# Broadcasting the mLSTM decay rows on GpSimd, folding the sample normaliser into the state matmul, and keeping one output weight in SBUF

## The chip, the cores and the metric

The kernel runs on one core of a Trainium2 chip. The metric is the device time of one launch in microseconds (us). A profiled execution carries timestamps for every instruction on the five engines: TensorE (PE, and PEld for its weight loads), VectorE (DVE), ScalarE (ACT), GpSimd (POOL) and SyncE (SP, which issues all DMAs here).

## The reference, cut to what matters

One layer of a hybrid decoder: 2048 prompt tokens plus 16 meta tokens (one sequence), and 32 sample tokens (8 streams of 4) that start from a stored state. An mLSTM group (4 heads of 128) and a sliding-window attention group (8 heads of 64) share one input projection and one output projection. The mLSTM part, in chunks of 128 tokens:

```python
def mlstm_chunk(state, q, k, v, log_i, log_f):
    c, n, m = state
    b = jnp.cumsum(log_f, axis=1)
    dmat = b[:, :, None, :] - b[:, None, :, :] + log_i[:, None, :, :]
    dmat = jnp.where(causal, dmat, -jnp.inf)
    inter = b + m[:, None, :]
    m_t = jnp.maximum(inter, jnp.max(dmat, axis=2))
    w = jnp.exp(dmat - m_t[:, :, None, :])
    s_inter = jnp.exp(inter - m_t)
    qk = jnp.einsum('bthd,bshd->btsh', q, k) * w
    num = jnp.einsum('btsh,bshd->bthd', qk, v) + jnp.einsum('bthk,bhkv->bthv', q, c) * s_inter[..., None]
    den = jnp.sum(qk, axis=2) + jnp.einsum('bthk,bhk->bth', q, n) * s_inter
    h = num / jnp.maximum(jnp.abs(den), jnp.exp(-m_t))[..., None]
    ...
    c_new = decay[..., None, None] * c + jnp.einsum('bsh,bshk,bshv->bhkv', w_state, k, v)
    n_new = decay[..., None] * n + jnp.einsum('bsh,bshk->bhk', w_state, k)

# per layer
mq, mk, mv, mo, mz, mi, mf, aq, ak, av, az = split_proj(hp @ w_in[l] + b_in[l])
mix = concatenate([y_m, y_a]) @ w_o            # y_m, y_a: the two groups, gated
out = layer_norm(DN_ALPHA * x + mix, g, b)
```

The prompt runs through `mlstm_chunk` 16 times with the carried state; the sample streams run once, from `state_mlstm_c` and `state_mlstm_n`.

## The kernel before, in words

All large products run on TensorE as pairs of float16 pieces (high and low parts, three products each), with the weights split on the chip. The kernel has two phases over the 16 chunks of 128 prompt tokens.

**Phase A** (`a_steps`, up to about 553 us of the profile) does, for chunk n: the gates (`a_gate`), the projections q, k, v, o with weights `w_q`, `w_k`, `w_v`, `w_o` (`a_proj`, 24 matmuls each, lines 296 to 299), the mLSTM itself, and the layer norm of the input two chunks ahead (`load_x`, `norm_x`). Everything phase B needs goes to DRAM (`xT_d`, `h_d`, `hn_d`). Between the steps, a generator `jobs` is advanced by `pace(0.8)`: it handles the sample streams (`d_prepare`, `d_head`, then the attention of the sample tokens), and prepares the weights of phase B, which are written to DRAM (`spill`) and read back later (`reload`).

**Phase B** (from about 553 us) does, for block n: projections aq, kv, az, z with reloaded weights `wr_aq`, `wr_kv`, `wr_az`, `wr_z`; the scores (`s_unit`, line 1259), the transposes of the probabilities by DMA, the product with the values (`s_pv`, lines 1301 and 1312); the output projection of an earlier block (`b_out`, line 1339) and the final layer norm.

The weights lie in the pool `wp` of 5 buffers of 2 MB, tag "w". In phase A four of them hold `w_q`, `w_k`, `w_v`, `w_o`; the fifth passes from one job to the next. PSUM has 8 banks: `pj` 2 (projections), `pt` 3, `po` 2, `px` 1 (sample jobs).

**The decay rows.** In `m_rows` (line 753) VectorE makes a tile `M` (`rM`) whose rows 0, 32, 64 and 96 hold one head each, with the tokens along the free axis. `m_weights` needs each of these rows on all 128 partitions: `Mb`, 128 x 4 x 128. Before, TensorE does that with a constant `sel` (one row of ones per head), four float32 matmuls into a `pt` bank (line 762). Readers of `Mb` are `ws` (line 772), the weights `wt` (line 776) and `SI` (ACT, line 778); `SI` scales the queries `qs` on POOL (line 787), after POOL has added the two halves of `qT` (line 786). `d_prepare` does the same once for the sample tokens (line 656).

**The sample normaliser.** In `d_head` the state `C` (8 streams, 128 x 128) and the normaliser `E.nS` (a column per stream) are separate, so every stream takes a matmul of 128 columns (line 702) and one of a single column (line 703).

Who orders the work: the text above gives the program, but a list scheduler with a model of the engines then sets the order of the instructions on each engine, and tiles are placed in buffers in that order. DMAs all go through SP's queue, in order.

Of the kernel before, what the change touches and what calls it, by code (L numbers as in the profile page):

```python
# [16 lines left out]
P = 128  # L17
# [24 lines left out]
def tile_hymba_step(  # L42
# [109 lines left out]

    G.load_library(library_config.standard)
    ones = cst.tile([P, P], F32, name="ones")
# [52 lines left out]
    swamask = cs[:, C_SWA:C_SWA + 2 * NW].rearrange("p (i k) -> p i k", k=NW)  # L207
    sel = cst.tile([P, H, P], F32, name="sel")
    G.memset(sel, 0.0)
    for h in range(H):  # L210
        G.memset(sel[32 * h:32 * h + 1, h], 1.0)
    Gf = [cst.tile([P, P], F32, name=f"Gf{i}") for i in range(2)]
# [434 lines left out]
    def d_prepare():  # L647

        E.nS, E.nn = ea.take(NS), ea.take(NS)
        dma(E.nS, st_n)  # L650
        E.em = ea.take(4)[:NS]
        A.activation(E.em, tok[:NS, 1, :], AF.Exp, scale=-1.0)
        Mb5 = ea.take(160).rearrange("p (h b s) -> p h b s", h=H, s=5)
        ps = pt([P, H, 40])
        for h in range(H):
            T.matmul(ps[:, h], sel[:, h], M5, start=True, stop=True)
        A.activation(Mb5.rearrange("p h b s -> p (h b s)"), ps.rearrange("p h t -> p (h t)"), AF.Copy)
        E.SI = ea.take(128).rearrange("p (h b s) -> p h b s", h=H, s=4)
        for h in range(H):
            V.tensor_tensor(E.SI[:, h], Mb5[:, h, :, 0:1].to_broadcast([P, 8, 4]), Mb5[:, h, :, 1:5], op=ALU.subtract)  # L660
        A.activation(E.SI, E.SI, AF.Exp)
        yield
        E.We = ea.take(128)[:NS].rearrange("p (h t) -> p h t", h=H)
        for h in range(H):
            V.scalar_tensor_tensor(v4(E.We[:, h]), Mb5[:NS, h, :, 1:5], tok[:NS, 0, h:h + 1], v4(scaus[:NS]),
                                   op0=ALU.subtract, op1=ALU.max)
        A.activation(E.We, E.We, AF.Exp, scale=-1.0)
        wa = Arena(wp.tile([P, 4096], F32, tag="w", name="da"))
        E.C = [wa.take(1024) for _ in range(2)]
        E.kz = wa.take(1024)[:NS]  # L670
        E.eh = wa.take(4 * 129)[:NS].rearrange("p (c d) -> p c d", d=129)
        E.Zq = wa.take(288)
        G.memset(E.Zq, 0.0)
        G.memset(E.eh[:, 2, 128:129], 1.0)
        E.qkT = ea.take(64).rearrange("p (c t) -> p c t", t=NS)
        E.A = ea.take(32)[:NS]
        E.g = ea.take(128)[:NS]
        E.kw = ea.take(128)[:NS]
        E.den = ea.take(1)[:NS]

    def d_head(h):

        eh, C = E.eh, E.C[h % 2]
        dma(eh[:, :, 0:P], e_d[0:NS, :, h * P:(h + 1) * P])
        C3 = v3(C)
        dma(C3, st_c[:, h].rearrange("b k v -> k b v"))
        ps = px([P, 2, P])
# [12 lines left out]
        for b in range(8):  # L700
            z = E.Zq[:, b * NS:(b + 1) * NS]
            T.matmul(ps[:NS, :128], z, C3[:, b], start=False, stop=False, skip_group_check=True)
            T.matmul(ps[:NS, 128:129], z, E.nS[:, b * H + h:b * H + h + 1], start=False, stop=(b == 7),
                     skip_group_check=True)
        yield
# [13 lines left out]
        dec = E.SI[:, h, :, 3]  # L719
        G.tensor_tensor(C3, C3, dec.unsqueeze(2).to_broadcast([P, 8, P]), op=ALU.mult)  # L720
        nn = E.nn.rearrange("p (b h) -> p h b", h=H)[:, h]
        V.tensor_tensor(nn, E.nS.rearrange("p (b h) -> p h b", h=H)[:, h], dec, op=ALU.mult)
        for b0 in range(0, 8, 3):
# [3 lines left out]
            for i in range(nb):  # L727
                T.matmul(ps[:, i], kz[:, b0 + i], eh[:, 2], start=True, stop=True, skip_group_check=True)
            V.tensor_tensor(C3[:, b0:b0 + nb], C3[:, b0:b0 + nb], ps[:, :nb, 0:P], op=ALU.add)
            V.tensor_tensor(nn[:, b0:b0 + nb], nn[:, b0:b0 + nb], ps[:, :nb, 128], op=ALU.add)  # L730
        dma(sc[:, h].rearrange("b k v -> k b v"), C3)
        if h == H - 1:
# [5 lines left out]
    def m_rows(n):  # L738
# [14 lines left out]
        V.scalar_tensor_tensor(M, r2[:, 1], carry.m, b, op0=ALU.subtract, op1=ALU.subtract)  # L753
        c.r2, c.M = r2, M
        carry.m = r2[:, 1, P - 1:P]

    def m_weights(n):
        c = ca[n]
        r2 = c.r2
        Mb = pt([P, H, P])  # L760
        for h in range(H):
            T.matmul(Mb[:, h], sel[:, h], c.M, start=True, stop=True)
        ptr = pt([P, 2, P])
# [273 lines left out]
    def x_out(i):  # L1037
        wB[f"o{i}"] = w = W()
        yield from prep_steps(w, f"o{i}", ahead[f"o{i}"], 512, mg=mg, sums=range(4))
        if i == 0:  # L1040
            fetch("o1")
        spill(w, f"o{i}")
        yield
# [38 lines left out]
    def a_steps(n):  # L1082
# [285 lines left out]
    for n in range(NCH - 1):  # L1368
# [135 lines left out]
```

## Time and profile before

| | us |
|---|---|
| three timed runs | 1099.37, 1101.61, 1102.27 (median 1101.61) |
| the profiled execution: its time | 1096.6 |
| its span, first to last instruction | 1094.8 |
| PE busy in the span | 1039.4 (95%) |
| DVE / ACT / POOL busy | 735.2 / 443.3 / 262.9 |
| mean granted TensorE clock | 0.984 of full speed |

In the rows of the profile, a line such as "L762 PE MATMUL pt<-rM,sel" names the line of the kernel, the engine, the operation, the tile written and the tiles read; after it stand the shapes and the count. Matmuls overlap one another, so the duration of one (285 ns, say) is longer than its distance to the next; what a matmul costs is read from the distance between starts.

### The profile page before, as it was taken

Reading aid. Unit: us, or ns where it says so; the run is one execution under the profiler, and the core shown is the slowest. Engines: PE = TensorE matmul, PEld = TensorE weight load, DVE = VectorE, ACT = ScalarE, POOL = GpSimd, SP = SyncE. Lnnn points to the kernel's source line nnn. Section 1 sums busy time; section 2 is a strip of 40 time slices with the busy share of each in tenths; the row PEclk is TensorE's granted clock in tenths of the full one; section 3 lists DMA queues with packets and bytes.
Section 4 is the critical chain, followed back from the end, with each engine's and each line's share of the span. In section 5 each row is a group of like instructions: output and inputs, shape, how many; then the busy total and the mean of one; then the engine's idle time right before and its main releaser. Section 6 shows DMA issues by size and latency. Waiting matters only on the chain.

```text
span 1094.8 us, 17806 instructions
## 1 busy us (share of the span) xinstructions
PE 1039.4 (95%) x6455; PEld 577.1 (53%) x6455; DVE 735.2 (67%) x2069; ACT 443.3 (40%) x1108; POOL 262.9 (24%) x270
## 2 busy tenths in 40 slices
PE   7969999999989999889998999999999999999986
PEld 3425565565556555445564554555555555555543
DVE  6769676776766777866655676566666656667664
ACT  5646333235434344562225344343344333344430
POOL 2113232121111111101311332233332233332222
PEclk9989999999999999999999999999999999999998
DMA  9746545445974568478585555656555464544552
GB/s 321 197 129 174 148 129 119 109 119 135 292 171 124 127 218 240 131 224 288 206 280 101 117 115 131 127 119 120 127 94 134 123 139 115 123 105 108 109 106 76
DMA packets 246098, 166.04 MB, mean 152 GB/s; under 512 B 207977, under 2 KB 220985, under 8 KB 244441
## 3 DMA queue, kind: packets, MB, share of 16 engines
q1 hardware_dynamic: 246010, 164.90, 58.9%
q8 instruction: 51, 0.84, 0.3%
q14 instruction: 37, 0.30, 0.1%
HBM read 70.32 MB, written 45.68 MB: 106 GB/s over the span
## 4 chain that ended last, share of the span: by engine, by line
PE 59%; DMA 15%; DVE 13%; ACT 6%; issue 5%; POOL 2%; SPq 1%; DVEq 0%; ACTq 0%; POOLq 0%
PE pj L1339 14%; PE pj L297 11%; PE pj L296 11%; PE pj L299 11%; DMA xT<-hl 3%; PE pt L1259 2%; DMA EE<-stg 2%; PE po L1312 2%; DMA stg<-in_dram 2%; DVE xs L380 1%; DMA stg<-hl 1%; DMA wd_z<-w_z 1%; DMA wd_o<-w_o 1%; ACT hl L321 1%; PE po L826 1%
## 5 line engine op out<-in xcount | busy, mean ns | idle before, releaser
L1339 PE MATMUL pj<-wr_o,EE 128*128 128x512 f16 x720 | 166.9, 381 | 3.0 <-DMA EE<-stg 1.5
L296 PEld LDWEIGHTS <-xT 128*128 128x128 f16 x992 | 97.9, 99 | 103.1 <-issue 6.9
L297 PEld LDWEIGHTS <-xT 128*128 128x128 f16 x992 | 97.8, 99 | 97.3 <-issue 6.8
L299 PEld LDWEIGHTS <-xT 128*128 128x128 f16 x992 | 96.8, 98 | 97.8
L1339 PEld LDWEIGHTS <-EE 128*128 128x128 f16 x720 | 70.5, 98 | 81.1 <-DMA EE<-stg 3.4
L325 POOL TENSOR_TENSOR lns<-lns,mhalf 128x1 f32<-128x1 f32 (+1 forms) x16 | 21.3, 1332 | 175.5 <-ACT lns L324 158.7
L1268 DVE TENSOR_TENSOR hl<-g,hl 128x512 f16<-128x512 f32 (+1 forms) x32 | 23.2, 724 | 49.1 <-ACT hl L1267 49.1
L1272 POOL TENSOR_TENSOR mhl<-g,mhl 128x32 f16<-128x32 f32 x32 | 18.8, 587 | 145.1 <-ACT mhl L1271 145.1
L296 PE MATMUL pj<-w_q,xT 128*128 128x512 f16 x120 | 47.1, 392 | 6.0 <-DMA xT<-hl 6.0
L1272 POOL TENSOR_TENSOR mhl<-SI,mhl 128x32 f16<-128x32 f32 x32 | 18.5, 578 | 139.1 <-ACT mhl L1271 139.1
L1266 ACT ACTIVATE g<-g,nb 128x272 f32<-128x272 f32 (+1 forms) x64 | 32.4, 507 | 46.3 <-DVE nb L1263 46.3
L296 PE MATMUL pj<-wr_z,xT 128*128 128x512 f16 x128 | 48.8, 381 | 0.0
L297 PE MATMUL pj<-wr_z,xT 128*128 128x512 f16 x128 | 48.7, 380 | 0.0
L296 PE MATMUL pj<-w_v,xT 128*128 128x512 f16 x120 | 46.3, 386 | 2.4 <-DVE q L431 2.4
L296 PE MATMUL pj<-wr_az,xT 128*128 128x512 f16 x128 | 48.5, 379 | 0.0
L296 PE MATMUL pj<-wr_aq,xT 128*128 128x512 f16 x128 | 48.5, 379 | 0.0
L297 PE MATMUL pj<-wr_aq,xT 128*128 128x512 f16 x128 | 48.5, 379 | 0.0
L297 PE MATMUL pj<-wr_az,xT 128*128 128x512 f16 x128 | 48.5, 379 | 0.0
L787 POOL TENSOR_TENSOR qs<-qs,SI 128x512 f32<-128x512 f32 x16 | 23.8, 1486 | 98.2 <-ACT SI L778 98.1
L297 PE MATMUL pj<-w_q,xT 128*128 128x512 f16 x120 | 47.0, 392 | 0.0
L297 PE MATMUL pj<-w_v,xT 128*128 128x512 f16 x120 | 46.5, 388 | 0.0
L297 PE MATMUL pj<-w_o,xT 128*128 128x512 f16 x120 | 46.5, 388 | 0.0
(459 smaller groups left out, 2510.4 us busy)
## 6 DMA issues: line engine op xcount, KB each, us to landing
stg<-in_dram SPq DMA_DIRECT2D x28, 512.0 KB
xs<-in_dram SPq DMA_DIRECT2D x16, 512.0 KB
h_d<-xs SPq DMA_DIRECT2D x16, 512.0 KB
xT_d<-xT SPq DMA_DIRECT2D x16, 512.0 KB
xs<-h_d SPq DMA_DIRECT2D x16, 512.0 KB
xT<-xT_d SPq DMA_DIRECT2D x16, 512.0 KB
out_dram<-xs SPq DMA_DIRECT2D x15, 512.0 KB
hn_d<-g SPq DMA_DIRECT2D x16, 258.0 KB
```

What stands on the lines that cost most here:

```text
L296: T.matmul(ps, xT[:, k, :], w.t[:, k, 0, :n], start=(k == 0), stop=False)
L297: T.matmul(ps, xT[:, k, :], w.t[:, k, 1, :n], start=False, stop=False)
L299: T.matmul(ps, xT[:, KT + k, :], w.t[:, k, 0, :n], start=False, stop=(k == KT - 1))
L321: A.activation(junk[:, 0:D], x, AF.Copy, accum_out=sm)
L325: G.tensor_tensor(rs, ve, mhalf[:rows, 0:1], op=ALU.pow)
L787: G.tensor_tensor(c.qs, c.qs, c.SI, op=ALU.mult)
L1259: T.matmul(ps[:, lo:], c.qT[:, h], kTs[:, 2 * (h // 4) + x, lo:], start=(x == 0), stop=(x == 1))
L1266: A.activation(p[:, i, lo:], p[:, i, lo:], AF.Exp, bias=nb[:, h:h + 1], accum_out=sums[:, h:h + 1])
L1268: V.tensor_tensor(hl[:, 1, 2 * q:2 * q + 2, lo:], p[:, :, lo:2 * P], hl[:, 0, 2 * q:2 * q + 2, lo:], op=ALU.subtract)
L1272: G.tensor_tensor(m[:, 1], p[:, :, 2 * P:], m[:, 0], op=ALU.subtract)
L1312: T.matmul(pso[:, h], l, r, start=False, stop=(i == len(last) - 1), skip_group_check=True)
L1339: T.matmul(ps, c.yT[:, a, :], w[:, k, t, :], start=(first and j == 0), stop=(last and j == len(mm) - 1))
```

## The change

The change has these parts.

1. The four selector matmuls per chunk become four `G.partition_broadcast` instructions on GpSimd (from row 32h of `M` to all partitions of `Mb`), issued in `m_rows`; `Mb` now lies in SBUF. The same in `d_prepare`, where the copy out of PSUM goes too. The constant `sel` goes. GpSimd loads another library of its routines at the start.
2. In `d_head` the state tile gets a 129th column per stream, which holds the normaliser. The product with the queries, the decay and the update then cover it in the same instructions; the single-column matmuls go.
3. `x` of chunk n+3 is loaded in step n, before the norm of n+2. Step n has one `yield` less, and the job generator is advanced at 0.92 instead of 0.8 per yield.
4. The second half of the output weights, `w_o1`, is not written to DRAM and reloaded: it stays in its `wp` buffer. `wr_aq` therefore has to take another buffer.
5. `b_out(0)` moves from the end of block 1 into block 2, ahead of that block's scores.

```diff
-    G.load_library(library_config.standard)
+    G.load_library(library_config.all_libraries[10])
...
-        ps = pt([P, H, 40])
         for h in range(H):
-            T.matmul(ps[:, h], sel[:, h], M5, start=True, stop=True)
-        A.activation(Mb5.rearrange("p h b s -> p (h b s)"), ps.rearrange("p h t -> p (h t)"), AF.Copy)
+            G.partition_broadcast(Mb5[:, h].rearrange("p b s -> p (b s)"), M5[32 * h:32 * h + 1], channels=P)
...
-        C3 = v3(C)
-        dma(C3, st_c[:, h].rearrange("b k v -> k b v"))
+        C3 = C.rearrange("p (b d) -> p b d", d=129)
+        dma(C3[:, :, 0:P], st_c[:, h].rearrange("b k v -> k b v"))
+        V.tensor_copy(C3[:, :, P], E.nS.rearrange("p (b h) -> p h b", h=H)[:, h])
...
-            T.matmul(ps[:NS, :128], z, C3[:, b], start=False, stop=False, skip_group_check=True)
-            T.matmul(ps[:NS, 128:129], z, E.nS[:, b * H + h:b * H + h + 1], start=False, stop=(b == 7),
-                     skip_group_check=True)
+            T.matmul(ps[:NS, :129], z, C3[:, b], start=False, stop=(b == 7), skip_group_check=True)
...
-        c.r2, c.M = r2, M
+        Mb = work("Mb", [P, H, P])
+        for h in range(H):
+            G.partition_broadcast(Mb[:, h], M[32 * h:32 * h + 1], channels=P)
+        c.r2, c.Mb = r2, Mb
...
-        Mb = pt([P, H, P])
-        for h in range(H):
-            T.matmul(Mb[:, h], sel[:, h], c.M, start=True, stop=True)
+        Mb = c.Mb
...
-        spill(w, f"o{i}")
+        if i == 0:
+            spill(w, "o0")
...
-            xs, carry.mark = load_x(n + 2)
-            yield
+            if n == 0:
+                carry.xs, carry.mark = load_x(2)
+                yield
+            xs = carry.xs
+            if n + 3 < NCH:
+                carry.xs, carry.mark = load_x(n + 3)
             xTs[n + 2] = norm_x(n + 2, xs)
...
-            if pace(0.8):
+            if pace(.92):
...
-    for nm in ("az", "z", "o0", "o1"):
+    for nm in ("az", "z", "o0"):
         reload(wB[nm], nm)
...
+        if n == 2:
+            b_out(0)
         s_start(n)
...
-        elif n < NCH - 2:
+        elif 1 < n < NCH - 2:
             b_out(n - 1)
```

Four places show what the scheduler makes of it. The new kernel is a few lines shorter: its lines 748, 779, 780 and 758 are lines 753 and after, 786, 787 and 765 of the kernel before; a POOL row "ISA Mb<-rM" is a broadcast.

On PE, in chunk 0 behind the projection v, before (line 762 and 656: the selectors; 765: transposes of other rows):

```order
L762 MATMUL pt<-rM,sel 128x128 x4
L765 MATMUL pt<-cs,r_712 128x128 x2
L656 MATMUL pt<-ea,sel 128x40 x4
L299 LDWEIGHTS xT
L299 MATMUL pj<-w_v,xT 128x512
```

and now:

```order
L296 LDWEIGHTS xT
L296 MATMUL pj<-w_v,xT 128x512
L758 MATMUL pt<-cs,r_706 128x128 x2
L790 LDWEIGHTS kT
L790 MATMUL pt<-qT,kT 128x128
```

The eight selector matmuls are gone from PE's row of work, and nothing stands in their place.

On POOL, in chunk 1 (717 and 720 before, 711 and 714 now, belong to the sample head; 325 and 322 are the power of the layer norm of x), before:

```order
L786 TENSOR_TENSOR qs<-qT 128x512
L717 TENSOR_TENSOR da<-ea,cs 32x1024
L325 TENSOR_TENSOR lns<-lns,mhalf 128x1
L720 TENSOR_TENSOR da<-da,ea 128x1024
L497 TENSOR_TENSOR hn<-hn,mhalf 32x1
L787 TENSOR_TENSOR qs<-qs,SI 128x512
```

and now:

```order
L779 TENSOR_TENSOR qs<-qT 128x512
L711 TENSOR_TENSOR da<-ea,cs 32x1024
L748 ISA Mb<-rM 128x128 x4
L780 TENSOR_TENSOR qs<-qs,SI 128x512
L322 TENSOR_TENSOR lns<-lns,mhalf 128x1
L714 TENSOR_TENSOR da<-da,ea 128x1032
```

The broadcasts stand behind the addition of the two halves of `qT`, which waits for a DMA transpose and for the previous chunk's use of `qs`; the multiplication by `SI`, which needs them, follows.

On SP, at the end of phase A, before (the first `qT` and `kT` are chunk 14's):

```order
L103 DMA wr_aq<-wd_aq 128x8192
L103 DMA wr_kv<-wd_kv 128x4096
L103 DMA xs<-ze_d 32x1024
L103 DMA xs<-h_d_149 128x1024
L103 DMA_TRANSPOSE qT<-qh 128x8x128
L103 DMA_TRANSPOSE kT<-kh 128x8x128
L103 DMA hn_d_178<-g 128x516
L103 DMA xT<-xT_d_133 128x2048
L103 DMA out_dram<-xs 32x1024
L103 DMA xs<-h_d_150 128x1024
L103 DMA wr_az<-wd_az 128x8192
```

and now (the `qT` and `kT` in these rows are chunk 15's):

```order
L103 DMA wr_aq<-wd_aq 128x8192
L103 DMA bias<-in_dram 128x512
L103 DMA_TRANSPOSE qT<-qh 128x8x128
L103 DMA hn_d_173<-g 128x516
L103 DMA out_dram<-r_5370 1x1 x4
L103 DMA wr_az<-wd_az 128x8192
L103 DMA bias<-in_dram 128x256
L103 DMA_TRANSPOSE kT<-kh 128x8x128
L103 DMA wr_z<-wd_z 128x8192
```

The reload of `wr_aq` stands where that of `wr_az` stood, behind chunk 15's projection q, whose buffer it takes; before, it stood a chunk earlier.

On ACT, in phase B when the scores of block 1 are made (1314 before, 1312 now: the result of `s_pv(0)`; 988 and 981: gates; 1266 and 1264: the exponentials of the scores), before:

```order
L1232 ACTIVATE At<-At,hnb,hn 128x128 x4
L988 ACTIVATE kw<-kT 128x512
L1314 ACTIVATE stg<-qT 128x512
L1266 ACTIVATE g,sums<-g,nb 128x272 x2
L1267 ACTIVATE hl<-g 128x512
```

and now:

```order
L1230 ACTIVATE At<-At,hnb,hn 128x128 x4
L1264 ACTIVATE g,sums<-g,nb 128x272 x2
L981 ACTIVATE kw<-qs 128x512
L1265 ACTIVATE hl<-g 128x512
L1269 ACTIVATE mhl<-g 128x32
L1312 ACTIVATE stg<-qT 128x512
```

The result of `s_pv(0)` now comes behind the first scores of block 1, not ahead of them.

More of the change, by code (lines that the diff above doesn't have):

```diff
@@ L207, in tile_hymba_step @@
     swamask = cs[:, C_SWA:C_SWA + 2 * NW].rearrange("p (i k) -> p i k", k=NW)
-    sel = cst.tile([P, H, P], F32, name="sel")
-    G.memset(sel, 0.0)
-    for h in range(H):
-        G.memset(sel[32 * h:32 * h + 1, h], 1.0)
     Gf = [cst.tile([P, P], F32, name=f"Gf{i}") for i in range(2)]
@@ L668, in d_prepare @@
         wa = Arena(wp.tile([P, 4096], F32, tag="w", name="da"))
-        E.C = [wa.take(1024) for _ in range(2)]
+        E.C = [wa.take(8 * 129) for _ in range(2)]
         E.kz = wa.take(1024)[:NS]
@@ L719, in d_head @@
         dec = E.SI[:, h, :, 3]
-        G.tensor_tensor(C3, C3, dec.unsqueeze(2).to_broadcast([P, 8, P]), op=ALU.mult)
-        nn = E.nn.rearrange("p (b h) -> p h b", h=H)[:, h]
-        V.tensor_tensor(nn, E.nS.rearrange("p (b h) -> p h b", h=H)[:, h], dec, op=ALU.mult)
+        G.tensor_tensor(C3, C3, dec.unsqueeze(2).to_broadcast([P, 8, 129]), op=ALU.mult)
         for b0 in range(0, 8, 3):
@@ L728, in d_head @@
                 T.matmul(ps[:, i], kz[:, b0 + i], eh[:, 2], start=True, stop=True, skip_group_check=True)
-            V.tensor_tensor(C3[:, b0:b0 + nb], C3[:, b0:b0 + nb], ps[:, :nb, 0:P], op=ALU.add)
-            V.tensor_tensor(nn[:, b0:b0 + nb], nn[:, b0:b0 + nb], ps[:, :nb, 128], op=ALU.add)
-        dma(sc[:, h].rearrange("b k v -> k b v"), C3)
+            V.tensor_tensor(C3[:, b0:b0 + nb], C3[:, b0:b0 + nb], ps[:, :nb], op=ALU.add)
+        dma(sc[:, h].rearrange("b k v -> k b v"), C3[:, :, 0:P])
+        A.activation(E.nn.rearrange("p (b h) -> p h b", h=H)[:, h], C3[:, :, P], AF.Copy)
         if h == H - 1:
@@ L759, in m_weights @@
         r2 = c.r2
-        Mb = pt([P, H, P])
-        for h in range(H):
-            T.matmul(Mb[:, h], sel[:, h], c.M, start=True, stop=True)
+        Mb = c.Mb
         ptr = pt([P, 2, P])
```

## The prediction

> **What bounds the kernel now.** I read the busy shares first, then the stretches, then PE's waits, then single places in the timeline.
>
> ```profile
> PE 1039.4 (95%) x6455; PEld 577.1 (53%) x6455; DVE 735.2 (67%) x2069; ACT 443.3 (40%) x1108; POOL 262.9 (24%) x270
> 20.00:553.00 533.00, 502.60 (x3016) 286.40 (x3015) 383.22 (x1088) 228.05 (x486) 95.86 (x71) 0.98 0.63 177
> 553.00:618.00 65.00, 61.05 (x367) 34.44 (x365) 41.45 (x149) 28.11 (x89) 11.25 (x21) 0.97 0.64 163
> 618.00:1040.00 422.00, 420.51 (x2774) 228.22 (x2773) 270.29 (x745) 166.24 (x485) 136.56 (x146) 1.00 0.54 119
> PE pj L296 <- DMA xT<-hl: 6.0, 1, 6.0
> PE px L728 <- DVE ea L707: 3.3, 3, 1.6
> PE pt L135 <- ACT SI L778: 2.9, 1, 2.9
> PE po L1312 <- DMA stg<-hl: 3.0, 2, 2.4
> ```
>
> The first row gives TensorE 95% of the span. The three stretches (length, then PE, PEld, DVE, ACT, POOL busy, then the granted TensorE clock) are phase A, the start of phase B, and steady phase B. PE is idle 30.4 us in phase A (533.0 less 502.6), 4.0 us at the start of B, and 1.5 us in the 422 us after it. The waits of PE (total, times, longest) are short and have many causes. So the time is PE's work plus a few stalls: a microsecond of matmul taken out of phase A is worth close to 502.6/533.0 = 0.94 us, and a stall is worth its length plus what the clock loses behind it. DVE, at 383 of 533 us, is the next engine, with room.
>
> **The selectors (part 1).** Their price is the distance between starts, not the 285 ns of one:
>
> ```profile
> L762 PE MATMUL pt<-rM,sel 128*128 128x128 f32 x128 | 17.9, 285 | 0.0
> 233.56 1.16 PE L762 MATMUL pt<-rM,sel 128*128 128x128 f32 x8
> 234.55 0.38 PE L765 MATMUL pt<-cs,r 128*128 128x128 f32 x2
> 94.58 0.98 PE L656 MATMUL pt<-ea,sel 128*128 128x40 f32 x8
> 95.62 0.83 PE L797 MATMUL pt<-qT,kT 128*128 128x128 f16 x12
> ```
>
> A chunk's block of 8 records (4 matmuls) starts at 233.56 and the next work at 234.55: 0.99 us. 128 records are 16 such blocks: 15.8 us. The sample block goes from 94.58 to 95.62: 1.0 us. Both leave PE's path for good: nothing takes their place in PE's order.
>
> **Their new price on POOL.** The trace has no broadcast. The nearest rows of POOL:
>
> ```profile
> L218 POOL MEMSET Gf<- 128x128 f32 x2 | 0.4, 205 | 0.0
> L846 POOL TENSOR_TENSOR kd<-kvu,kd 128x128 f16<-128x128 f32 x32 | 15.4, 499 | 6.3 <-ACT kd L844 6.1 <-POOL hl L1274 0.2
> L325 POOL TENSOR_TENSOR lns<-lns,mhalf 128x1 f32<-128x1 f32 (+1 forms) x16 | 21.3, 1332 | 175.5 <-ACT lns L324 158.7 <-ACT am L767 16.9
> 16.81 0.60 POOL L325 TENSOR_TENSOR lns<-lns,mhalf 48x1 f32<-48x1 f32 x1 [9.56 <-ACT lns L324]
> ```
>
> A fill of 128x128 is 0.2 us, an operation with two inputs of that size 0.5 us, a software routine (a power of one element) up to 1.33 us. One broadcast is thus between 0.2 and 1.33 us; I take 0.5 us, the row with the same shape, so 2.0 us for four. What stands behind them is the reader:
>
> ```profile
> 531.21 0.34 DVE L753 SCALAR_TENSOR_TENSOR rM<-r,r,rb 128x128 f32<-128x128 f32 x1
> 535.97 0.16 DVE L772 TENSOR_TENSOR ws<-am,pt 128x4 f32<-128x4 f32 x1 [1.36 <-ACT am L767]
> 264.08 0.34 DVE L753 SCALAR_TENSOR_TENSOR rM<-r,r,rb 128x128 f32<-128x128 f32 x1
> 270.61 0.15 DVE L772 TENSOR_TENSOR ws<-am,pt 128x4 f32<-128x4 f32 x1
> 279.39 1.78 POOL L786 TENSOR_TENSOR qs<-qT 128x512 f32<-128x512 f16 x1 [13.37 <-DMA qT<-qh]
> ```
>
> `M` is ready at 531.55 and its first reader runs at 535.97: 4.4 us go to PE's turn and the evictions today. Four broadcasts of 0.5 us need 2.0, so they hide in it; at 1.33 us (5.3) VectorE would wait 0.9 us a chunk. If they hide, the cost is zero; that cover ends at 1.1 us each. The load of POOL's routine library, new too, comes once at the start, where POOL waited 9.56 us ahead of its first power (the row at 16.81); I count 0. DVE reads `Mb` from SBUF instead of PSUM; the 0.34 us of line 753, with its inputs in SBUF, is the size of that, off PE's path.
>
> The Trainium skill, page "GPSIMD Engine Reference", section "Specifications", says GpSimd shares its SBUF interfaces with VectorE and contends with vector instructions that use two ports or two SBUF inputs. The trace agrees as far as it goes: the same power took 0.60 us at 16.81 and 1.33 us on average. By that rule a broadcast would come to about 1.1 us (an estimate, 0.5 times 1.33/0.60), four to 4.4 us, just the cover, and the sum would stay but without margin.
>
> **PSUM (part 1).** `Mb` held one of three `pt` banks until `SI` was made. Once that stopped PE:
>
> ```profile
> 485.18 0.49 PE L135 MATMUL pt<-dg,ones 128*128 128x128 f32 x2 [2.90 <-ACT SI L778]
> 480.00:490.00 10.00, 6.80 (x39) 3.04 (x38) 8.35 (x22) 6.97 (x21) 2.60 (x2) 0.83 0.64 184
> PE pt L511 <- ACT SI L778: 0.4, 1, 0.4
> ```
>
> 2.9 and 0.4 us of waiting, and in that stretch the clock is 0.83 over 10 us, so 1.7 us lost: together 5.0 us. Between 0 (another bank or VectorE is late next, DVE being busy 8.35 of those 10 us) and 5.0, I take half, 2.5.
>
> **The normaliser (part 2).**
>
> ```profile
> L703 PE MATMUL px<-ea,da 128*32 128x1 f32 x64 | 6.3, 168 | 0.0
> 126.16 0.20 PE L703 MATMUL px<-ea,da 128*32 128x1 f32 x2
> 126.22 0.39 PE L702 MATMUL px<-da 128*32 128x128 f32 x2
> ```
>
> A column matmul (two records) delays the next one by 0.06 us: 32 of them are 1.9 us. A 129th column adds under 1% to the other 32. Small vector additions go and one small copy per head comes, off the path. The sample jobs have slack, so their side is zero.
>
> **x further ahead, and the pace (part 3).**
>
> ```profile
> ACT hl L321 <- DMA xT<-hl: 42.2, 11, 7.2
> ACT hl L321 <- DMA xs<-in_dram: 2.0, 1, 2.0
> ```
>
> The norm of x waits for the tile `hl`, whose transpose must be out (42.2 us in 11 times), not for x (2.0 us, once, at the start). The load ahead buys at most 2.0 us, and I count 0. The jobs advance by 9 x 0.92 = 8.3 per chunk instead of 10 x 0.8 = 8: no change.
>
> **o1 kept (part 4).** One write and one reload of 2 MB go; PE waits for neither. What is moved is `wr_aq`:
>
> ```profile
> 506.45 0.32 SPq L103 DMA_DIRECT2D wr_aq<-wd_aq x1
> 531.86 0.38 PE L299 MATMUL pj<-w_q,xT 128*128 128x512 f16 x1
> 533.81 0.37 SPq L103 DMA_DIRECT2D wr_az<-wd_az x1
> 553.11 0.38 PE L296 MATMUL pj<-wr_aq,xT 128*128 128x512 f16 x1
> 540.00:550.00 10.00, 9.54 (x55) 5.56 (x53) 6.24 (x27) 1.31 (x3) 1.15 (x1) 1.00 1.18 333
> ```
>
> It used to be issued 46.7 us ahead of its use. Now it can go only when chunk 15's last `w_q` matmul is out (531.86; the transfer that took that buffer was issued at 533.81), 19.3 us ahead of 553.11. At 333 GB/s, the rate of the last row, 2.1 MB need 6.3 us. Hidden, with 13 us to spare; `wr_az`, `wr_z` and the `kT` transpose queue behind it, but the sum of four reloads after 533.81 is what it was. Cost 0.
>
> **b_out(0) later (part 5).**
>
> ```profile
> 593.09 0.61 PE L1301 MATMUL po<-Vm,mT 128*128 128x256 f16 x4 [0.57 <-DMA mT<-mhl]
> 596.43 0.82 PE L1312 MATMUL po<-vd,stg 128*128 128x64 f16 x12 [2.38 <-DMA stg<-hl]
> 590.00:600.00 10.00, 7.06 (x52) 4.00 (x51) 6.90 (x27) 3.58 (x10) 2.59 (x5) 0.83 0.39 74
> 600.00:610.00 10.00, 8.99 (x46) 4.20 (x44) 6.60 (x20) 5.91 (x19) 1.08 (x3) 1.00 0.51 117
> ```
>
> Block 0's values waited 2.4 us for their transpose; PE idles 2.9 + 1.0 us in these 20 us, and the clock of 0.83 takes 1.7: 5.6 us at most. With scores and projections now ahead of that product, most of it should go, but the scheduler's other moves may bring some back: between 0 and 5.6, I take 2.8.
>
> Both stalls above are followed by a lower clock after PE waits of 2.9 and 2.4 us. The Trainium skill, page "TensorE: Matmul & The Clock Gate", section "What's actually happening", puts the fall to half clock after an idle window of about 3.4 us. Here shorter waits did it, so the trace decides; by the page the two clock terms (1.7 each, of which half is counted) would not be there and the sum would be 1.7 us smaller.
>
> **The sum.** 15.8 + 1.0 + 1.9 = 18.7 us of matmul, times 0.94 is 17.6; plus 2.5 and 2.8: 22.9 us. The profiled execution took 1096.6 (span 1094.8 and 1.8 around it), so it would take 1073.7. The median of the runs, 1101.61, is 5.0 above that execution; I keep that distance and predict 1078.7 us for the median, 2.1% less.
>
> **Rivals.**
>
> *Phase A does not shorten by what PE loses.* For: 30.4 us idle there and DVE 72% busy, with waits such as line 728's on the vector engine. Against: no cause exceeds 6.0 us. With half the matmul time coming back as waits, the gain is 9.4 + 5.3 = 14.7: 1086.9. Chance 0.12.
>
> *The broadcasts queue behind a late transpose.* POOL takes its work in order, and the addition ahead of them (786) waits for `qT`. In chunk 6 it ran at 279.39 to 281.17, while `ws` ran at 270.61. With the broadcasts behind it, `ws` would come at 283.2, 12.6 us later, with VectorE's queue behind it, PE's evictions in that, and 1.7 us of clock. Against: in the chunk of 531.21 the addition had long run, and where `qT` is late, the scores that need it are late anyway. Once in full: 22.9 - 14.3 = 8.6, 1093.0; twice, no change. Chance 0.10.
>
> *Slower: the broadcast is a slow routine.* Beyond 1.1 us each VectorE waits in every chunk. The gain is eaten at 22.9/16 = 1.4 us a chunk over the cover of 4.4: 1.45 us each. At 2.5 us it is 16 x (10.0 - 4.4) = 90 us: 1168. For: 1.33 us for one element of a power. Against: a row is copied, nothing is computed, and 0.2 to 0.5 us is what 128x128 costs. Chance 0.06.
>
> **How the numbers follow.** The forecast with its own range has 0.72: from 1068 (both stalls gone in full, all 18.7 kept, and 4 us more of phase A's other waits) to 1086. I take the change as measurable from 0.3%, 3.3 us. The first rival is 0.11 faster and 0.01 same (its worst form, in which all 22.9 us come back as waits); the second is 0.05 faster, 0.04 same, 0.01 slower; the third is 0.06 slower. Faster 0.72 + 0.11 + 0.05 = 0.88; same 0.01 + 0.04 = 0.05; slower 0.01 + 0.06 = 0.07. The range 1068 to 1093 holds the forecast, the first rival and the milder half of the second.
>
> **What would show it.** Right: no matmul into `Mb`, PE's busy time about 18 us lower, all of it before 553; groups of four broadcasts of about 2 us; no PE wait on `SI`; no wait of line 1312's product at the start of B. Wrong: VectorE's `ws` or `wt` waiting for POOL; PE waits in phase A well over 30 us; `wr_aq` late at the start of B, with a clock drop behind it.

## The result and the profile after

| | before | after |
|---|---|---|
| median of the timed runs | 1101.15 us (4 runs) | 1086.67 us (1085.56 to 1088.16, 4 runs) |
| the profiled execution: its time, its span | 1096.6, 1094.8 | 1085.56, 1083.5 |
| PE busy / DVE busy / POOL busy | 1039.4 / 735.2 / 262.9 | 1024.0 / 743.2 / 283.3 |

The ratio after to before is 0.9871, 95% interval 0.9851 to 0.9891: 1.3% faster, 14.5 us between the medians, where 22.9 were forecast. It is inside the range, and almost exactly where the first rival stood (half the matmul time comes back as waits, 1086.9); which part brought the gain is another question, and the experiments answer it otherwise than the sum did.

First the page's busy row and the three stretches of the changed kernel, in the columns shown of before.

```profile
PE 1024.0 (95%) x6255; PEld 558.2 (52%) x6255; DVE 743.2 (69%) x2057; ACT 445.6 (41%) x1111; POOL 283.3 (26%) x333
20.00:553.00 533.00, 495.69 (x2840) 273.10 (x2841) 391.60 (x1086) 235.58 (x502) 119.00 (x140) 0.97 0.62 170
553.00:618.00 65.00, 64.68 (x443) 37.85 (x441) 42.40 (x144) 28.71 (x88) 11.90 (x23) 1.00 0.66 163
618.00:1040.00 422.00, 420.62 (x2765) 227.26 (x2763) 274.59 (x754) 162.84 (x478) 134.71 (x143) 1.00 0.54 119
```

At the start of phase B PE is idle 0.3 us now (4.0 before) at the full clock. In phase A it is idle 37.3 us (533.0 less 495.69), where it was 30.4 before: matmul left, waits came. PE's longest new waits, the wait of the rows' first reader on ScalarE (total, times, longest), and the broadcast's row on the page (busy, mean ns of one, idle of POOL ahead of it):

```profile
PE po L639 <- DVE da L682: 5.7, 1, 5.7
PE pt L735 <- DVE Gf L478: 4.7, 1, 4.7
ACT SI L771 <- POOL Mb L748: 31.1, 11, 4.5
L748 POOL PARTITION_BROADCAST Mb<-rM x64 | 29.4, 559 | 112.5 <-DVE rM L745 102.4
L748 POOL PARTITION_BROADCAST Mb<-rM x64: 422/427/4983, 90.3 to 538.8; - x64
```

The last row (least, median and most ns of one) says that a broadcast takes 0.43 us, and that one took 4.98 us. The reader that waits for the rows is `SI` on ACT, in 11 of 16 chunks; VectorE's `ws` never waits for POOL.

To compare kernels whose instructions stand in different orders, I split PE's time by the distances between starts: *work* is every matmul at the median distance of its kind over all the kernels here, *lost* is all the rest from the first to the last matmul (waits and slow clock). Both are worked out from one profiled execution of each kernel. With kinds by shape alone, or by shape, tiles and line, the two columns move by up to 3 us, alike in all kernels; differences between kernels move by less than 1.

| stretch (us) | lost before | lost after |
|---|---|---|
| up to 120 | 23.0 | 29.9 |
| 120 to 300 | 9.7 | 11.8 |
| 300 to 460 | 13.7 | 14.0 |
| 460 to 552 | 7.8 | 11.5 |
| 552 to 620 | 6.1 | 0.5 |
| 620 to the end | 9.0 | 5.9 |
| all | 69.2 | 73.6 |

Work went from 1012.6 to 995.3 us, 17.3 less. The first matmul starts 1.4 us later. 17.3 less 4.4 less 1.4 is the 11.5 us by which the span is shorter (11.3 by the profile). Of the 13.0 us more that are lost up to 552, 10.6 lie in two stretches, up to 120 (a place near 100 us) and from 460 to 552 (a place near 512); from 552 on, 8.7 less are lost.

**Near 100.** From the timeline after, DVE, POOL, ACT and PE in chunk 0 (a bracket is the idle time ahead and who ended it), then the stretch after, then two rows of before:

```profile
90.15 3.67 DVE L271 SCALAR_TENSOR_TENSOR w_o<-stage,cols,w_o 128x1024 f16<-128x1024 f32 x3
93.74 1.28 DVE L376 SCALAR_TENSOR_TENSOR xs<-xs,lns,gb 128x1024 f32<-128x1024 f32 x1
90.33 5.89 POOL L748 PARTITION_BROADCAST Mb<-rM  x4 [12.39 <-DVE rM L745]
96.25 0.63 ACT L771 ACTIVATE SI<-Mb 128x512 f32<-128x512 f32 x1 [4.54 <-POOL Mb L748]
97.08 0.68 ACT L305 ACTIVATE g<-px,cols 48x512 f32<-48x512 f32 x1
97.80 0.96 DVE L306 TENSOR_TENSOR g<-g,bias 48x512 f32<-48x512 f32 x1 [2.78 <-ACT g L305]
101.15 0.73 DVE L312 SCALAR_TENSOR_TENSOR vaug<-px,cols,g 48x512 f32<-48x512 f32 x1
102.03 2.06 PE L639 MATMUL po<-vaug,kw 16*128 16x129 f32 x8 [5.74 <-DVE da L682]
95.00:115.00 20.00, 14.26 (x83) 8.29 (x81) 15.16 (x43) 7.89 (x19) 4.93 (x9) 0.74 0.72 189
```

```profile
91.67 0.68 ACT L308 ACTIVATE g<-px,cols 48x512 f32<-48x512 f32 x1
98.77 0.60 ACT L778 ACTIVATE SI<-pt 128x512 f32<-128x512 f32 x1
95.00:115.00 20.00, 18.74 (x127) 11.19 (x126) 16.48 (x48) 8.06 (x21) 6.58 (x6) 1.00 0.88 219
```

The first broadcast is issued at 90.33 and ends only when VectorE's weight splits and the operation behind them are out (95.02). ACT now has `SI` ahead of `g`, the eviction for the meta tokens; `SI` waits 4.54 us for the rows, so `g` runs at 97.08 (before: 91.67, with `SI` at 98.77, behind it), `vaug` at 101.15, and PE stands 5.74 us in front of its product (the profile names `da`, which ended 0.08 us after `vaug`); the clock falls to 0.74 over 20 us. Two things meet here: the late rows, and an order on ACT that puts `g` behind their reader.

**Near 512.** The rows after, and for comparison a pair of before that the prediction did not look at:

```profile
508.91 2.34 POOL L1167 TENSOR_TENSOR xs<-xs,gb 32x1024 f32<-32x1024 f32 x1 [0.92 <-DVE ls L470]
508.95 2.32 DVE L471 TENSOR_TENSOR ls<-ls 128x4 f32<-128x4 f32 x1
511.32 2.35 POOL L1168 TENSOR_TENSOR xs<-xs,gb 32x1024 f32<-32x1024 f32 x1
511.50 2.20 DVE L473 TENSOR_SCALAR ls<-ls 128x4 f32<-128x4 f32 x1
517.22 0.45 PE L735 MATMUL pt<-cs,Gf 128*128 128x128 f32 x1 [4.74 <-DVE Gf L478]
510.00:530.00 20.00, 15.26 (x88) 8.39 (x87) 14.19 (x39) 5.26 (x15) 7.27 (x8) 0.83 0.33 87
```

```profile
521.39 2.33 POOL L1169 TENSOR_TENSOR xs<-xs,gb 32x1024 f32<-32x1024 f32 x1 [0.92 <-DVE ls L474]
521.42 2.34 DVE L475 TENSOR_TENSOR ls<-ls 128x4 f32<-128x4 f32 x1
```

An addition of 128x4 lasts 2.3 us, to the end of POOL's product, after as before; so does a `TENSOR_SCALAR` with a single tensor input (2.20). After, this falls on the chain of gates that PE waits for.

### The profile page after: what moved, and what is told of

Same layout as the page of the kernel before. It is cut to its first block, busy times and chain, and to the rows that moved or that the text cites. A ratio compares the mean times of both kernels' runs of the same rounds, so it can differ in the third digit from the quotient of the medians.

```text
span 1083.5 us, 17427 instructions
## 1 busy us (share of the span) xinstructions
PE 1024.0 (95%) x6255; PEld 558.2 (52%) x6255; DVE 743.2 (69%) x2057; ACT 445.6 (41%) x1111; POOL 283.3 (26%) x333
## 4 chain that ended last, share of the span: by engine, by line
PE 59%; DMA 15%; DVE 13%; ACT 5%; issue 3%; SPq 2%; POOL 1%; DVEq 0%; ACTq 0%; POOLq 0%
PE pj L1337 13%; PE pj L293 12%; PE pj L294 12%; PE pj L296 11%; DMA xT<-hl 6%; PE pt L1257 2%; SPq L103 2%; PE po L1310 2%; DMA stg<-hl 1%; DMA EE<-stg 1%; ACT hl L318 1%; DMA wd_z<-w_z 1%; DVE hl L1266 1%; DMA wd_o<-w_o 1%; DVE xs L377 1%
## 5 line engine op out<-in xcount | busy, mean ns | idle before, releaser
L1337 PE MATMUL pj<-wr_o,EE 128*128 128x512 f16 x360 | 87.4, 379 | 0.9 <-DMA EE<-stg 0.8
L1337 PE MATMUL pj<-w_o,EE 128*128 128x512 f16 x360 | 80.3, 379 | 0.2 <-DVE qs L1224 0.2
L748 POOL PARTITION_BROADCAST Mb<-rM x64 | 29.4, 559 | 112.5 <-DVE rM L745 102.4
L779 POOL TENSOR_TENSOR qs<-qT 128x512 f32<-128x512 f16 x16 | 23.2, 1451 | 111.9 <-DMA qT<-qh 57.9
L1270 POOL TENSOR_TENSOR mhl<-SI,mhl 128x32 f16<-128x32 f32 x32 | 18.3, 572 | 126.3 <-ACT mhl L1269 126.3
L293 PE MATMUL pj<-w_v,xT 128*128 128x512 f16 x120 | 46.2, 385 | 0.4 <-DVE q L428 0.4
```

The lines of the kernel that those rows point to most:

```text
L293: T.matmul(ps, xT[:, k, :], w.t[:, k, 0, :n], start=(k == 0), stop=False)
L748: G.partition_broadcast(Mb[:, h], M[32 * h:32 * h + 1], channels=P)
L779: G.tensor_tensor(c.qs, c.qT[:, 0], c.qT[:, 1], op=ALU.add)
L1270: G.tensor_tensor(m[:, 1], p[:, :, 2 * P:], m[:, 0], op=ALU.subtract)
L1337: T.matmul(ps, c.yT[:, a, :], w[:, k, t, :], start=(first and j == 0), stop=(last and j == len(mm) - 1))
```

## The experiments

| kernel | ratio to before [95%] | median us | work | lost | of it to 120 | 460-552 | 552-620 |
|---|---|---|---|---|---|---|---|
| before | 1 | 1098.0 to 1101.2 by set | 1012.6 | 69.2 | 23.0 | 7.8 | 6.1 |
| the changed kernel | 0.9871 [0.9851, 0.9891] | 1086.67 | 995.3 | 73.6 | 29.9 | 11.5 | 0.5 |
| part 1 alone | 0.9983 [0.9969, 0.9997] | 1097.51 | 997.6 | 83.8 | 29.6 | 11.6 | 10.6 |
| part 5 alone | 0.9947 [0.9925, 0.9968] | 1092.24 | 1012.6 | 64.4 | 22.3 | 9.2 | 5.2 |
| parts 1 and 5 | 0.9924 [0.9897, 0.9952] | 1088.73 | 997.6 | 73.0 | 29.1 | 10.2 | 1.4 |
| all but part 1 | 0.9842 [0.9813, 0.9871] | 1080.85 | 1010.5 | 55.3 | 23.7 | 4.9 | 3.8 |
| all but part 3 | 0.9870 [0.9843, 0.9897] | 1084.95 | 995.3 | 73.6 | 30.0 | 12.6 | 0.2 |
| all but part 4 | 0.9881 [0.9855, 0.9907] | 1085.85 | 995.3 | 74.4 | 29.6 | 8.6 | 1.8 |
| all but part 5 | 0.9983 [0.9963, 1.0004] | 1096.80 | 995.3 | 86.2 | 31.1 | 12.3 | 9.9 |
| changed, broadcasts twice | 0.9906 [0.9883, 0.9929] | 1087.98 | 995.2 | 76.0 | 31.1 | 10.2 | 0.4 |
| changed, chunk 0 by selectors | 0.9823 [0.9799, 0.9848] | 1080.18 | 996.1 | 68.9 | 25.2 | 6.1 | 1.0 |
| changed, sample norm later | 0.9818 [0.9796, 0.9840] | 1080.20 | 995.3 | 70.1 | 30.1 | 4.2 | 2.1 |
| both of these | 0.9788 [0.9756, 0.9820] | 1074.94 | 996.1 | 63.2 | 26.2 | 1.1 | 1.3 |

The rows come from four sets of runs, each beside the kernel before, whose median was 1098.0 to 1101.2 us by set. So medians of different sets are not subtracted here: differences between kernels are taken from the ratios, where 0.001 is 1.1 us.

A scheduler sets the order, so each of these edits also moves instructions far from it; differences of a few us in a stretch that an edit does not touch are of that kind.

**1. The two engines by themselves** (`micro`: nothing of the kernel, blocks of POOL and VectorE work; the scheduler let neighbouring blocks run into each other, so pairs are read as they fell).

```
def bc():     4 x G.partition_broadcast(Mb[h], src[32*h:32*h+1])          # 128x128
def mul():    3 x G.tensor_tensor(zz[:32], big[:32], bigb[:32], mult)     # 32x1024
def split():  6 x V.scalar_tensor_tensor(fo, big, sc1, f2)                # two inputs in SBUF
def scale(): 12 x V.tensor_scalar(tz, big[:, 0:512], sc1)                 # one input in SBUF
def evict(): 10 x V.scalar_tensor_tensor(pf, ps, sc1, big[:, 0:512])      # PSUM and SBUF
def tiny2(): 24 x V.tensor_tensor(to, tiny[:, 0:4], tiny[:, 4:8], add)
...                                                                       # operators of the others left out
```

> This kernel computes nothing of the reference: after loads it runs blocks in which GpSimd does four broadcasts (128x128) or three products (32x1024, two inputs), each alone and then beside a run of VectorE work of one kind: the weight split (float32 and float16 inputs in SBUF), a scaling (one input in SBUF), an eviction (PSUM and SBUF inputs), additions of 128x4 with two inputs, and products of 128x4 with one. Theory A (the two engines shut each other out of SBUF): a broadcast alone takes 0.43 us, the first one too; beside six splits of 1.2 us the first broadcast ends only with the last split, after some 7 us; beside the eviction it stays at 0.43 us; an addition of 128x4 beside a product of GpSimd lasts as long as that product, 2.3 us instead of 0.15. Theory B (first use of the routine is slow): the first broadcast of the program takes about 5 us with VectorE idle, and all later ones take 0.43 us, whatever VectorE does. Theory C (plain sharing of bandwidth): every broadcast beside the splits takes up to twice as long, 0.5 to 0.9 us, and none takes several us.

By line (least, median, most ns of one), and a stretch of the timeline:

```profile
L205 POOL PARTITION_BROADCAST Mb<-src x28: 422/427/1493, 5.7 to 31.2; - x28
L213 DVE SCALAR_TENSOR_TENSOR fo<-big,sc,f x12: 1269/1272/3351, 5.6 to 76.7; 128x1024 f16<-128x1024 f32 x12
L217 DVE TENSOR_SCALAR tz<-big,sc x24: 361/475/2257, 5.3 to 84.4; 128x512 f32<-128x512 f32 x24
L225 DVE TENSOR_TENSOR to<-tiny x48: 142/149/1996, 57.8 to 96.9; 128x4 f32<-128x4 f32 x48
L221 DVE SCALAR_TENSOR_TENSOR pf<-pj,sc,big x20: 734/736/740, 37.9 to 92.3; 128x512 f32<-128x512 f32 x20
10.36 3.94 POOL L205 PARTITION_BROADCAST Mb<-src  x12
60.44 0.74 DVE L221 SCALAR_TENSOR_TENSOR pf<-pj,sc,big 128x512 f32<-128x512 f32 x1
60.66 2.33 POOL L209 TENSOR_TENSOR zz<-big,bigb 32x1024 f32<-32x1024 f32 x1
61.10 1.92 DVE L225 TENSOR_TENSOR to<-tiny 128x4 f32<-128x4 f32 x1
```

A broadcast costs 0.43 us, twelve in a row 3.94, some 0.3 from start to start. Broadcasts that met a split of 1.27 us took 1.37 to 1.49, to 0.3 us after its end; a split that met a product of POOL took 3.35; an addition of 128x4 took 1.92 instead of 0.15, to the product's end at 63.0. A scaling, with one tensor input in SBUF, goes the same way: 0.36 us at the least, 1.90 to 2.26 beside the products. Only the eviction, with an input in PSUM, stayed at 0.74 beside the products. This is theory A: for operations whose tensor inputs lie in SBUF, two or one, one engine waits until the other's instruction is over. Sharing (C) would stretch both a little. A slow first use (B) falls: the program's first broadcast took 1.46 us, beside a split, and that of the changed kernel 0.34 (at 76.95, 40 elements a row). The Trainium skill, page "SBUF — State Buffer", section "Terms", says the same of the port pair that VectorE and GpSimd share: a lock, held for a full instruction, on which the loser blocks; the rows above agree. Six splits in a row beside a broadcast did not come up here, nor an eviction beside a broadcast, nor, for its length, a product of 128x4 with one input beside one of POOL. That a broadcast is kept out by several operations in a row, the changed kernel showed with 4.98 us, over four.

**2. Part 1 alone** (before, with the broadcasts and without the selectors).

> The kernel before with part 1 alone (broadcasts for selectors). Sum theory: 16.8 us of matmul go, times 0.94 is 15.8, and the stalls of before stay as they are: 1085 us, ratio 0.9855. Theory A (broadcasts shut out by VectorE and the waits behind them give back 6 to 8 us in the chunks where they collide): 1091 to 1094 us, ratio 0.991 to 0.993. If parts 2 to 5 carry the gain instead, it is above 0.995.

Measured 0.9983: 15.0 us less work by the starts, and 14.6 us more lost. Nearly all of the sum's 15.8 is gone again: theory A, with 6 to 8 us, is too small by half, and the third reading, above 0.995, holds. The losses are 6.6 more up to 120, 3.8 from 460 to 552, and 4.5 at the start of phase B, where PE waits for block 0's output projection:

```profile
553.00:618.00 65.00, 56.80 (x335) 30.96 (x333) 39.98 (x139) 25.74 (x81) 10.98 (x21) 0.95 0.60 145
603.11 3.17 PE L1334 MATMUL pj<-wr_o,EE 128*128 128x512 f16 x7 [5.82 <-DMA EE<-stg]
85.36 5.24 POOL L750 PARTITION_BROADCAST Mb<-rM  x4 [6.68 <-DVE cols L125]
91.94 0.61 ACT L773 ACTIVATE SI<-Mb 128x512 f32<-128x512 f32 x1
97.36 0.67 DVE L305 TENSOR_TENSOR g<-g,bias 48x512 f32<-48x512 f32 x1
```

In chunk 0 its four broadcasts took 5.24 us, too, beside three splits of `w_v` and a pass of the layer norm. But here they did not reach PE: they ended at 90.6, and ACT, busy with the operations ahead of it, took `SI` at 91.94 without waiting. PE's wait of 4.9 us in chunk 0 has VectorE's order behind it: the addition to `g` stands behind four splits of `w_o` (one of them 2.33 us long, beside a product of POOL) and runs at 97.36 (in the kernel before at 94.58). And from 460 to 552 PE waits 4.8 us for the rows `r`, with no VectorE operation of 128x4 held up by the sample tokens' norm. So in this kernel most of what is lost is not shown to come from the exclusion.

**3. Chunk 0 by selectors** (changed kernel).

```
-        Mb = work("Mb", [P, H, P])
-        for h in range(H): G.partition_broadcast(...)
+        if n > 0: (the broadcasts)
...
+        if n == 0:
+            Mb = pt([P, H, P])
+            for h in range(H):
+                T.matmul(Mb[:, h], sel[:, h], c.M, start=True, stop=True)
```

> The changed kernel, but chunk 0's rows are spread by four selector matmuls as before. In the changed kernel the first broadcast of chunk 0 lasted 4.98 us beside VectorE's weight splits, PE waited 5.7 us behind it and ran at half clock to 110 us. Theory A: that wait and the clock loss go (5.7 + 4.9), one block of selectors (1.0) comes back: 8 to 10 us faster than the changed kernel, 1077 to 1079 us, ratio 0.978 to 0.980. Rival (VectorE is late there anyway, or the order made by the scheduler brings another wait): within 3 us of the changed kernel, ratio 0.984 to 0.990.

0.9823 against 0.9871, some 5 us faster than the changed kernel, less than the 8 to 10 expected and outside the rival's range. PE's wait of 5.7 us shrank to 1.2, `g` stands ahead of `SI` again, and the clock of the stretch came back from 0.74 to 0.91:

```profile
92.91 0.68 ACT L309 ACTIVATE g<-px,cols 48x512 f32<-48x512 f32 x1 [0.30 <-PE px L307]
99.71 0.60 ACT L781 ACTIVATE SI<-pt 128x512 f32<-128x512 f32 x1
95.00:115.00 20.00, 18.76 (x120) 11.09 (x118) 14.97 (x40) 6.65 (x18) 4.54 (x5) 0.91 0.80 198
```

The loss up to 120 fell by 4.7, that from 460 to 552 by 5.4 (another order), and others grew. The edit mends two things at once, the late rows and the order of `g` and `SI`; broadcasts with `g` ahead of `SI` were not run.

**4. The sample tokens' last norm later** (changed kernel; `if n == 0` becomes `if n == 4` ahead of `z = work("xs", ...)`, `final(z, NS, y_s)`, and the `elif` behind it an `if`).

> The changed kernel, but the last layer norm of the sample tokens (two products of 32x1024 on GpSimd, 2.35 us each, run at 508.9 to 513.7) stands four blocks later in the program. Theory A: VectorE's operations of 128x4 for the gates no longer last 2.3 us, PE's wait of 4.7 us at 512 and the half clock behind it (3.4) go: 5 to 8 us faster than the changed kernel, 1079 to 1082 us, ratio 0.980 to 0.983. Rival (the gates are late for another reason, or another wait takes the place): within 2 us of it, ratio 0.985 to 0.989.

0.9818, some 6 us faster, as theory A had it. The 128x4 operation takes 0.16 us, and PE has no gap in the stretch:

```profile
521.26 0.16 DVE L471 TENSOR_TENSOR ls<-ls 128x4 f32<-128x4 f32 x1
510.00:530.00 20.00, 20.00 (x132) 11.61 (x130) 11.17 (x42) 5.56 (x15) 3.76 (x9) 1.00 0.34 118
```

**5. Both mends together.**

> The changed kernel with chunk 0's rows by selectors and the sample tokens' last layer norm four blocks later. Theory A (two separate collisions of VectorE and GpSimd, worth 6.5 us each as measured one by one): 13 us faster than the changed kernel, 1073 to 1075 us, ratio 0.975 to 0.978. Rival (the gains are chance of the order, and another wait takes the place): 1078 to 1082, ratio 0.980 to 0.984.

0.9788, some 9 us faster than the changed kernel by the ratios (10.4 by the spans of the profiled executions), where the two one by one give 11: a little short of theory A's range, and beyond the rival's. The losses are 26.2 up to 120 and 1.1 from 460 to 552. The two places are not wholly separate: chunk 0's edit alone had already lowered the second to 6.1. It is the fastest kernel of the study.

**6. Part 5 undone** (changed kernel, `b_out(0)` back at its place).

> The changed kernel with part 5 undone: block 0's output projection stands again one block earlier. Theory D (part 5 is what took the stalls away at the start of phase B, and these grow when phase A gets shorter, as in the kernel with part 1 alone, where PE waited 5.8 us for that projection's input and 10.6 us were lost from 552 to 620): 6 to 10 us slower than the changed kernel, 1093 to 1097 us, ratio 0.994 to 0.997. Rival (the x load, the pace or the kept weight did it): within 2 us of the changed kernel, ratio 0.985 to 0.989.

0.9983: some 12 us slower than the changed kernel, more than theory D gave. 9.4 of it is lost from 552 to 620, and the stall is that of part 1 alone:

```profile
606.82 3.59 PE L1337 MATMUL pj<-wr_o,EE 128*128 128x512 f16 x8 [5.76 <-DMA EE<-stg]
```

**7. Part 3 undone, part 4 undone** (changed kernel).

> The changed kernel with part 3 undone: x loaded when the step needs it, jobs paced by 0.8 of ten steps. Prediction on record (part 3 is worth nothing): within 3 us of the changed kernel, ratio 0.984 to 0.990. Rival (part 3 carries the difference between the change as a whole, 14 us, and part 1 alone, 2 us, in phase A): 5 to 8 us slower, ratio 0.991 to 0.994.

> The changed kernel with part 4 undone: the second output weight written and reloaded again, so that wr_aq is reloaded early. Prediction on record (worth nothing, both are hidden): within 3 us of the changed kernel, ratio 0.984 to 0.990. Rival (the traffic of 4 MB costs at the start of phase B): 4 us slower or more, ratio above 0.990.

0.9870 and 0.9881: both as predicted, worth nothing in this company.

**8. Part 5 alone, and parts 1 and 5.**

> The kernel before with part 5 alone (block 0's output projection later). Theory D (it removes all that is lost at the start of phase B, 6.0 us from 552 to 620, and nothing else): 5 to 6 us faster than before, ratio 0.9945 to 0.9955. Prediction on record: 2.8 us, ratio 0.9975. Rival (it is worth as much as in the changed kernel, 10 us, with or without part 1): ratio 0.990 to 0.991.

> The kernel before with parts 1 and 5 together. Part 1 alone gave 0.9983 and undoing part 5 in the changed kernel cost 10 us. Theory D (what part 1 takes out of phase A is handed back at the start of phase B unless part 5 is there; parts 3 and 4 are worth nothing, part 2 at most 1.9 us): ratio 0.987 to 0.990, 1086 to 1089 us. Rival (parts 2 to 4 carry a share that shows only in company): ratio 0.991 or above.

Part 5 alone: 0.9947, as theory D had it in size, though not in place: only 0.9 of the 4.8 us less lost are from 552 to 620, some 4 come after 620. Parts 1 and 5: 0.9924, so parts 2 to 4 carry some 0.5% on top, of which part 2's work (2.3 us) is 0.2%; here the rival held. The two profiled executions, 1085.59 and 1085.56 us, do not show that difference.

**9. The broadcasts twice** (changed kernel, each broadcast of the chunks issued two times).

> The changed kernel with each broadcast of the prompt's chunks issued twice: 64 more, 0.29 us from start to start, 18.8 us more work on GpSimd in all, 1.2 us a chunk. Prediction on record (the broadcasts hide as long as four take less than 4.4 us a chunk): within 3 us of the changed kernel, ratio 0.984 to 0.990. Rival (they lie on the path, each chunk waits for them; doubling them also doubles the collisions with VectorE): 10 to 19 us slower, ratio 0.996 to 1.004.

0.9906, some 4 us slower than the changed kernel: just above the first range, which the interval reaches into, and short of the rival, for 64 more broadcasts and 18.8 us more of POOL. In an ordinary chunk they do hide, nearly. PE's loss up to 120 rose by 1.2.

**10. Part 1 undone** (changed kernel with the selectors).

> The changed kernel with part 1 undone: the rows spread by selector matmuls again, all other parts kept. Matmul sum on record: 16.8 us of PE work come back, times 0.94: 1102 us, ratio 1.002. Theory A (with them the collisions of broadcasts and VectorE go, 6.5 us measured in chunk 0): 9 to 10 us slower than the changed kernel, 1096 us, ratio 0.996. Rival (part 5 carries the whole gain, the broadcasts none): 1086 to 1090 us, ratio 0.987 to 0.991.

0.9842: beyond the rival, no slower than the changed kernel but some 3 us faster by the ratios, which is not clear of the noise (the intervals overlap from 0.985 to 0.987).

```profile
PE 1031.0 (96%) x6391; PEld 571.7 (53%) x6391; DVE 731.0 (68%) x2057; ACT 442.8 (41%) x1112; POOL 253.5 (24%) x270
20.00:553.00 533.00, 506.58 (x3001) 287.09 (x3000) 385.92 (x1084) 232.91 (x502) 90.61 (x72) 0.98 0.63 174
92.06 0.69 ACT L309 ACTIVATE g<-px,cols 48x512 f32<-48x512 f32 x1
508.09 2.20 DVE L477 TENSOR_SCALAR ls<-ls 128x4 f32<-128x4 f32 x1
```

PE does 15.2 us more work than in the changed kernel and loses 18.3 less. Of these, 6.2 lie up to 120 and 6.6 from 460 to 552; another 3.5 lie after 620, where neither kernel has a broadcast: a matter of the order. `g` in chunk 0 runs at 92.06. The sample tokens' norm still holds up a 128x4 operation (the row at 508.09), and PE waits 3.1 us behind it: that collision does not need the broadcasts. DVE is busy 12.2 us less (731.0 against 743.2, 2057 instructions in both), but only 5.7 of it between 20 and 553 (385.92 against 391.60), where the broadcasts run.

## Why the prediction held, and where it did not

**The sign and the range held; the main term did not.** Part 1 was to bring 15.8 + 1.0 us of matmul times 0.94, and 2.5 of PSUM relief. The work went as counted (15.0 us by the starts), but part 1 itself is worth 1.9 us alone, and nothing that the runs show beside the other parts (0.9842 without it, 0.9871 with it). That the total still fell inside the range is in part luck: this term was forecast far too large, that of `b_out(0)` too small. The step that failed is "four of 0.5 us need 2.0, so they hide in it [4.4 us] ... the cost is zero". The price of one was right (0.43), and in 12 of 16 chunks all four took no more, so in an ordinary chunk they nearly hide. Two things were wrong. The duration was taken as the instruction's own: a broadcast that meets VectorE's long operations with inputs in SBUF lasts as long as these. And the cover was read from `ws` on VectorE, 4.4 us later, while the first reader now was `SI` on ACT (31.1 us of waiting), in chunk 0 with the meta tokens' eviction behind it. Up to 120 us every kernel with broadcasts in chunk 0 lost 29.1 to 31.1 us of PE, the three without broadcasts 22.3 to 23.7; selectors in chunk 0 alone brought it to 25.2 and 26.2. That the loss goes with the broadcasts is shown; that it comes through the late rows the timeline shows for the changed kernel, while with part 1 alone it comes through VectorE's order. What the removed matmuls had covered of PE's waits was not measured by itself.

**The sentence on the contention** had the right two engines and the wrong form: it made the broadcast 1.33/0.60 times longer on average, and found it just covered. It is a lock, not a slope. Rows of before showed that and were not read: the addition of 128x4 in 2.34 us at 521.42, and behind the mean of 1.33 us for the power these durations (least, median, most):

```profile
L325 POOL TENSOR_TENSOR lns<-lns,mhalf x16: 547/1322/3945, 16.8 to 482.0; 128x1 f32<-128x1 f32 x15, 48x1 f32<-48x1 f32 x1
```

The power of 3.95 us ran from 91.72 to 95.67, beside the splits of `w_o` that later held up the broadcast, and ended 0.4 us after four VectorE operations in a row were out (95.25); with VectorE idle, at 323.35, it took 0.55.

**The PSUM term (2.5) can't be found as a gain.** The wait on `SI` went, but the loss from 460 to 552 rose from 7.8 to 11.5. In the changed kernel the sample tokens' norm fell on the gates' chain there, and moving that norm away left 4.2 lost. With part 1 alone the loss rose as much (11.6) without that, and with the selectors back and the norm where it was it is 4.9; so no run shows a gain that belongs to the bank.

**The column (1.9): right in size.** 2.3 us of work by the comparison of parts 1 and 5 with the changed kernel (1.4 to 2.3 by how the kinds are sorted); it was not run alone.

**x, the pace, the kept weight (0): right,** each by undoing it; no wait for `wr_aq` appeared.

**b_out(0) later (2.8 of at most 5.6): too small.** The stretch itself went from 6.1 lost to 0.5, the full bound. Alone the part is worth 0.53% (5.8 us), though the stretch then only goes to 5.2, and some 12 us in the changed kernel, because with part 1 that projection would wait 5.8 us for its transpose. The bound was read from the stall as it stood before, not from what it becomes when the work ahead of it is shorter.

**The distance of 5.0 us** between profiled execution and median was 1.1 after. Profile against profile the change brought 11.0 us, median against median 14.5.

**The rivals.** The first gave the right number by the right kind of cause, waits in phase A, but it has them spread; two places carried most, and the number is a coincidence: 13.0 us came back up to 552, not 9.4, and 8.7 were won after it, not 5.3. The second appeared once, mildly:

```profile
198.13 1.15 POOL L779 TENSOR_TENSOR qs<-qT 128x512 f32<-128x512 f16 x1 [7.36 <-DMA qT<-qh]
```

In that chunk `M` was ready at 196.42 and the broadcasts began at 199.26, 2.8 us later, behind this addition; in the 15 others they began 0.1 us after `M`, and no wait of PE names them. (In its price, twice in full would be 5.7 us slower by its own figures, not no change.) The third's price was far off as a steady one.

**What stays open.** All parts but the first give 0.9842, part 5 alone 0.9947. Of the 11 us between them some 2 are part 2's work; parts 3 and 4 were worth nothing when undone in the changed kernel, and whether they are worth something without broadcasts, or the scheduler's order was lucky, was not tried. Nor was it settled why in the changed kernel one broadcast was kept out by four of VectorE's operations in a row, while in the kernel with part 1 alone one got in after each. How much of chunk 0's loss is the late rows and how much the order on ACT was not separated either. The kernel with selectors and the sample norm later was not run.

## What to carry to other kernels

Work moved from PE to GpSimd is not priced by its duration there but by the VectorE operations it can meet: look in the trace for small VectorE operations that last as long as a GpSimd one beside them, and for a reader of the moved result at the head of a queue with unrelated work behind it. Microseconds taken out of a 95% busy engine can come back as waits: with part 1 alone 15.0 went and 14.6 came back. Undoing each part of a change in the finished kernel shows which part pays, as far as the scheduler's new order lets one tell, and here it was not the one with the largest count. And a stall's gain is bounded by what the stall becomes after the other parts, not by its size before.

## What the runs showed of the hardware

In these runs GpSimd's instructions and VectorE's operations with their tensor inputs in SBUF, two or one, kept each other out for whole instructions: an addition of 0.15 us became 1.92, a scaling of 0.36 became 2.26, a split of 1.27 became 3.35, a broadcast of 0.43 became 4.98, while an eviction from PSUM kept its 0.74 beside GpSimd's products. Which of them gets in when VectorE's operations follow one another was not settled. The broadcast itself is cheap, 0.43 us for 128x128 and some 0.3 us apart in a row, and its first use cost nothing visible (0.34 us in the changed kernel).
